# Two chained matrix products with a GELU between them: a first product opened by slices of the contraction, warm-up matmuls, and one load queue

## The chip, the cores and the metric

The kernel runs on one NeuronCore of a Trainium2 chip. The metric is the device time of one execution in microseconds. Three executions of the kernel before took 157.47, 232.58 and 156.98 us; their median is 157.47 us.

The engines by the names that the profile gives them: PE is TensorE (matmuls and transposes), with PEld for its loads of the stationary operand; DVE is VectorE, ACT is ScalarE, POOL is GpSimd, and SP issues DMAs (SPq is its queue). Matmuls write to PSUM, and DVE or ACT move their results from there to SBUF.

## The reference

```python
m, k, n, p = 1024, 1024, 2048, 1024     # a: m x k, b: k x n, c: n x p, all float32
h = np.matmul(a, b)
h = 0.5 * h * (1 + np.tanh(np.sqrt(2 / np.pi) * (h + 0.044715 * h ** 3)))
return np.matmul(h, c).astype(np.float32)
```

The inputs have 4.19 MB (a), 8.39 MB (b) and 8.39 MB (c); the output has 4.19 MB.

## The kernel before

All inputs come in as float32, are cast to bf16 on the core, and both products run in bf16 with sums in float32. One matmul multiplies a 128x128 stationary block by a 128x512 moving block. The first product has 16 column tiles of b (n), 8 slices of the contraction (k) and 1024 rows of a, so 16 x 8 x 2 = 256 matmuls; the second has 8 row tiles, 2 halves of the output's columns and 16 slices of its contraction, again 256.

The rows of a are worked in two chunks of 512 (the loop over mc). For each chunk `load_a_chunk` loads four row tiles of 128 x 1024 (tile sta, L51), casts them on ACT (a_bf, L53), and turns them by 64 transposes of 128x128 in the whole kernel (L60, by a matmul against an identity matrix) and as many DVE copies (L61) into aT, which has one 128x512 tile per slice of k. In the first chunk only, b is loaded in four slices of 512 columns, each as eight pieces of 128x512 (stb, L68) that ACT casts into b_sb (L69), and c comes in 16 row tiles (stc, L73, issued by POOL) that DVE casts (L74). For every column tile nt, eight matmuls (L90) sum one PSUM tile over k, and ACT applies the GELU and writes hT (L93). Then the second product runs over the chunk's four row tiles and two column halves: 16 matmuls (L100) sum one PSUM tile over all 16 tiles of hT, DVE copies it out (ot, L104) and SP stores it (L105). With that the chunk is done and the next one begins, with its own transposes.

The program is written in this order, but a scheduler places the instructions of each engine's queue: on PE it mixes transposes of one slice with matmuls of up to three open PSUM tiles. SP carries the loads of a and b and the stores; POOL carries those of c. Every load waits until its staging buffer (six each for sta and stb, three for stc) has been cast.

## Time and profile before

| what | value |
|---|---|
| three executions | 157.47, 232.58, 156.98 us (median 157.47) |
| span of the profiled execution | 157.0 us |
| mean granted TensorE clock | 0.946 |
| PE busy | 125.8 us (80%) |
| ACT busy | 47.6 us (30%) |
| DVE busy | 33.7 us (21%) |
| read from HBM, written | 20.97 MB, 4.19 MB |

The span runs from the first to the last instruction of one profiled execution on the one core. Nothing lies around it that the times show: it equals the lowest of the three times, 156.98 us, within its rounding. A row of a group of instructions gives the line, the engine, the operation, the tiles (out<-in), how often it ran, the busy time and the mean of one in ns, and then the idle time ahead of it with what ended it. A row of a stretch gives for each engine its busy microseconds and, in brackets, its instructions; then the granted clock as a share of full speed, the mean busy share of the 16 DMA engines and the GB/s that they moved. Matmuls overlap in their pipeline, so the mean duration of a matmul is longer than the time from one to the next.

### The profile page before, as it was taken

What the parts mean: (1) busy time and instruction counts of PE and PEld (TensorE: products, weight loads), DVE (VectorE), ACT (ScalarE), POOL (GpSimd) and SP (SyncE); (2) the same over time, 40 slices, a digit from 0 to 9 for tenths busy, and PEclk for the clock granted to TensorE, in tenths of its full rate; (3) what the DMA queues carried; (4) which work ended last, traced back from release to release, by engine and by line L of the source; (5) the groups of instructions that cost most, each with busy time, mean ns of one, the idle gap of its engine ahead of it and who ended that gap; (6) DMA issues with size and microseconds to landing.
All of it is one profiled execution on the core that took longest, in us unless ns stands there. A gap on an engine that the chain in (4) does not pass through costs nothing.

```text
span 157.0 us, 1522 instructions
## 1 busy us (share of the span) xinstructions
PE 125.8 (80%) x565; PEld 56.4 (36%) x576; DVE 33.7 (21%) x96; ACT 47.6 (30%) x74; POOL 9.3 (6%) x22
## 2 busy tenths in 40 slices
PE   0104952729994699999999979999999999999990
PEld 0001421213441244444444434444444444444440
DVE  0022664423113100011122146600000002111111
ACT  3534734497563995300000000053343310000000
POOL 6010121221210000000000000000000000000000
PEclk9999997555999789999999999999999999999999
DMA  5999999999999930011111120000000001122111
GB/s 177 406 381 316 362 338 413 397 399 401 395 399 398 410 155 2 0 67 71 67 67 69 69 103 30 0 4 0 0 0 0 0 4 67 67 84 112 72 67 67
DMA packets 10375, 25.26 MB, mean 161 GB/s; under 512 B 1152, under 2 KB 1152, under 8 KB 10368
## 3 DMA queue, kind: packets, MB, share of 16 engines
q1 hardware_dynamic: 8064, 16.78, 29.0%
q0 software_dynamic: 2304, 8.39, 13.6%
q8 instruction: 4, 0.07, 0.2%
q14 instruction: 3, 0.02, 0.1%
HBM read 20.97 MB, written 4.19 MB: 160 GB/s over the span
## 4 chain that ended last, share of the span: by engine, by line
PE 62%; DMA 26%; ACT 5%; DVE 2%; SPq 2%; issue 1%
PE ps L100 35%; DMA stb<-in_b_dram 26%; PE ps L90 24%; ACT b_sb L69 3%; PE pt L60 2%; ACT hT L93 2%; SPq L51 1%; DVE aT L61 1%; DVE ot L104 1%; ACT L93 1%; SPq L68 1%
## 5 line engine op out<-in xcount | busy, mean ns | idle before, releaser
L90 PE MATMUL ps<-aT,b_sb 128*128 128x512 bf16 x250 | 66.8, 410 | 8.9 <-ACT hT L93 7.1
L100 PE MATMUL ps<-c_sb,hT 128*128 128x512 bf16 x251 | 55.3, 379 | 0.3
L90 PEld LDWEIGHTS <-b_sb 128*128 128x128 bf16 x256 | 26.2, 103 | 48.7 <-issue 20.3
L100 PEld LDWEIGHTS <-hT 128*128 128x128 bf16 x256 | 25.0, 98 | 30.2
L93 ACT ACTIVATE hT<-ps 128x512 bf16<-128x512 f32 x32 | 18.6, 594 | 56.7 <-PE ps L90 55.6
L104 DVE COPY ot<-ps 128x512 f32<-128x512 f32 x16 | 11.1, 692 | 81.8 <-PE ps L100 81.8
L60 PE MATMUL pt<-ident,a_bf 128*128 128x128 bf16 x64 | 13.3, 240 | 18.4 <-ACT a_bf L53 11.7
L69 ACT ACTIVATE b_sb<-stb 128x512 bf16<-128x512 f32 x32 | 19.8, 629 | 15.1 <-DMA stb<-in_b_dram 14.8
L74 DVE CAST c_sb<-stc 128x1024 bf16<-128x1024 f32 x16 | 11.1, 692 | 27.2 <-DMA stc<-in_c_dram 27.1
L61 DVE COPY aT<-pt 128x128 bf16<-128x128 bf16 x64 | 12.5, 220 | 11.4 <-PE pt L60 10.8
L60 PEld LDWEIGHTS <-a_bf 128*128 128x128 bf16 x64 | 6.7, 107 | 17.7 <-ACT a_bf L53 12.3
L73 POOL DMA_DIRECT2D stc<-in_c_dram x16 | 8.6, 539 | 35.1 <-DVE aT L61 23.0
L53 ACT ACTIVATE a_bf<-sta 128x1024 bf16<-128x1024 f32 x8 | 8.4, 1054 | 6.3 <-DMA sta<-in_a_dram 6.3
L53 ACT ACT_TABLE_LOAD x1 | 1.3, 1283 | 0.7 <-PEq L120 0.7
L93 ACT ACT_TABLE_LOAD x1 | 1.3, 1283 | 0.0
masks.py:199 POOL TENSOR_SCALAR_AFFINE_SELECT ident<-ident 128x128 bf16<-128x128 bf16 x1 | 0.3, 306 | 0.1
masks.py:197 POOL MEMSET ident<- 128x128 bf16 x1 | 0.2, 205 | 0.3 <-POOLq L120 0.3
L120 POOL MEMSET const-float32-0.0<- 128x1 f32 x1 | 0.1, 99 | 0.2 <-issue 0.2
L120 POOL MEMSET const-bfloat16-1.0<- 128x1 bf16 x1 | 0.1, 102 | 0.0
L120 POOL MEMSET const-uint8-127<- 128x1 uint8 x1 | 0.1, 102 | 0.0
L120 POOL MEMSET const-float32-1.0<- 128x1 f32 x1 | 0.1, 99 | 0.0
## 6 DMA issues: line engine op xcount, KB each, us to landing
stc<-in_c_dram POOLq DMA_DIRECT2D x16, 512.0 KB, 6.8
stb<-in_b_dram SPq DMA_DIRECT2D x32, 256.0 KB, 7.5
sta<-in_a_dram SPq DMA_DIRECT2D x8, 512.0 KB, 7.9
out_dram<-ot SPq DMA_DIRECT2D x16, 256.0 KB, 2.0
```

The lines of the kernel that those rows point to most:

```text
L51: nc.sync.dma_start(out=st, in_=a[ds(mc * MC + mt * 128, 128), :])
L53: nc.scalar.activation(t, st, AF.Copy)
L60: nc.tensor.transpose(pt, a_bf[mt][:, ts(kt, 128)], ident)
L61: nc.vector.tensor_copy(at[:, ts(mt, 128)], pt)
L68: nc.sync.dma_start(out=st, in_=b[ts(kt, 128), ts(j, BS)])
L69: nc.scalar.activation(b_sb[kt][:, ts(j, BS)], st, AF.Copy)
L73: nc.gpsimd.dma_start(out=st, in_=c[ts(nt, 128), :])
L74: nc.vector.tensor_copy(c_sb[nt], st)
L90: nc.tensor.matmul(ps, b_sb[kt][:, ts(nt, 128)], aT[kt], start=(kt == 0), stop=(kt == KT - 1))
L93: nc.scalar.activation(h, ps, AF.Gelu_apprx_tanh)
L100: nc.tensor.matmul(ps, hT[nt][:, ts(mt, 128)], c_sb[nt][:, ts(pc, PC)], start=(nt == 0), stop=(nt == NT - 1))
L104: nc.vector.tensor_copy(ot, ps)
```

## The change

The kernel's body is rewritten, and the engines' queues now follow the written order (manual_schedule).

- The opening. a is loaded by slices of k: one DMA brings 128 columns of all 1024 rows (a_st, 512 KB, L64; the first slice in two halves, L60 and L62), followed by the same slice of the first 384 columns of b (b0_st, 192 KB, L65; the first of them on ACT's queue, L61). DVE casts the slice of a in two halves (L84, L85), ACT casts that of b (L86), PE makes eight transposes into two PSUM tiles of 128x512 (L90), and one wide copy each takes these to aT, on DVE for the first 512 rows (L92) and on ACT for the rest (L94). The function mm0 then adds this slice to six PSUM tiles at once (three column tiles by two halves of the rows, L79). All eight slices done, ACT applies the GELU to the six tiles (L120).
- The rest of the first product. mm1 works the column tiles 3 to 15, eight matmuls for each half of the rows (L126), with the GELU behind (L128). All of aT stays in SBUF, so both halves of the rows use a column tile of b when it is there. The second product starts when the first is done for all rows (L149); the last row tile's second half of columns is worked in two parts of 256.
- The loads. One queue, SP's, carries all loads but one in the order of use: the slices of the opening, b's column tiles 3, 4 and 5 singly (pieces of 128 columns), 6 and 7 together, 8 to 11, 12 to 15 (L107), then c by 1 MB (L113). DVE casts these (L108, L114), from four shared staging buffers of 1 MB.
- Ahead of it all DVE zeroes a tile (L45), PE makes seven matmuls of it that nothing reads (L73), and ACT runs one GELU on a column of it (L70).

How the queues change, at three places. The first is SP's queue from its start. A name such as a_st or sta is a staging tile, in_a_dram is the input a; the last numbers are the shape moved by one DMA. Before:

```order
L51 DMA sta<-in_a_dram 128x1024 x4
L68 DMA stb<-in_b_dram 128x512 x32
L51 DMA sta<-in_a_dram 128x1024 x4
L105 DMA out_dram<-ot 128x512 x16
```

Now, from the opening's second-last slice on:

```order
L64 DMA a_st<-in_a_dram 128x8x128
L65 DMA b_st<-in_b_dram 128x384
L64 DMA a_st<-in_a_dram 128x8x128
L65 DMA b_st<-in_b_dram 128x384
L107 DMA st<-in_b_dram 128x8x128 x3
L107 DMA st<-in_b_dram 128x8x256
L107 DMA st<-in_b_dram 128x4x512 x4
L113 DMA st<-in_c_dram 128x2x1024 x8
L142 DMA out_dram<-ot 128x512 x15
```

All of a now stands ahead of the wide loads of b, in pieces of 128 columns (512 bytes), and c's loads have moved from POOL's queue behind those of b.

The second place is PE's queue near the start; the weight load ahead of each matmul is left out. pt is a transposed block, ps a PSUM tile of the first product. Before, a block of four row tiles is turned and two or three sums are open:

```order
L60 MATMUL pt_156<-ident_58,a_bf_131 128x128
...
L90 MATMUL ps1_278<-aT_133,b_sb_93 128x512
...
L60 MATMUL pt_160<-ident_58,a_bf_119 128x128
...
L60 MATMUL pt_163<-ident_58,a_bf_123 128x128
...
L90 MATMUL ps1_264<-aT_146,b_sb_94 128x512
```

Now, behind the transposes of the second slice of k (aT0_1 is slice 0, second half of the rows; aT1_0 is slice 1, first half):

```order
L90 MATMUL pt_219<-ident_86,ab_209 128x128
...
L79 MATMUL ps_185<-aT0_1_92,b_sb_107 128x512
...
L79 MATMUL ps_187<-aT0_1_92,b_sb_107 128x512
...
L79 MATMUL ps_189<-aT0_1_92,b_sb_107 128x512
...
L79 MATMUL ps_184<-aT1_0_93,b_sb_107 128x512
...
L79 MATMUL ps_186<-aT1_0_93,b_sb_107 128x512
...
L79 MATMUL ps_188<-aT1_0_93,b_sb_107 128x512
```

Six sums are open, and each slice of a gives eight transposes and six matmuls; the three matmuls of the older slice stand between the transposes and the matmuls that need the newest copy.

The third place is DVE's queue, at the end of the opening. Before, the copies of single transposed blocks alternate with c's casts:

```order
L74 CAST c_sb<-stc 128x1024
L61 COPY aT<-pt 128x128 x4
L74 CAST c_sb<-stc 128x1024
L61 COPY aT<-pt 128x128
L74 CAST c_sb<-stc 128x1024 x9
```

Now the casts of a and one wide copy per slice, and behind them the casts of b and c:

```order
L84 CAST ab<-a_st 128x512
L85 CAST ab<-a_st 128x512
L92 COPY aT_0_105<-pt 128x512
L108 CAST b_sb<-st 128x8x128 x3
L108 CAST b_sb<-st 128x8x256
L108 CAST b_sb<-st 128x4x512 x4
L114 CAST c_sb<-st 128x2048 x8
```

No cast of c stands between the copies that PE waits for any more.

The added lines of the diff, cut to its core (the removed ones are the body printed above):

```diff
-    MC = 512
-    PC = 512
-    BS = 512
-    NSL = N // BS
+    MT = M // 128
+    H = 512
+    N0 = 3
+    W0 = N0 * 128
+    av = a.rearrange("(mt p) k -> p mt k", p=128)
+    bv = b.rearrange("(kt p) n -> p kt n", p=128)
+    cv = c.rearrange("(nt p) q -> p nt q", p=128)
+    ctx.enter_context(tc.manual_schedule())
     consts = ctx.enter_context(tc.tile_pool(name="consts", bufs=1))
-    ident = consts.tile([128, 128], BF16)
+    astage = ctx.enter_context(tc.tile_pool(name="astage", bufs=4))
+    abf = ctx.enter_context(tc.tile_pool(name="abf", bufs=3))
+    keep = ctx.enter_context(tc.tile_pool(name="keep", bufs=1))
+    b0stage = ctx.enter_context(tc.tile_pool(name="b0stage", bufs=4))
+    stage = ctx.enter_context(tc.tile_pool(name="stage", bufs=4))
+    opool = ctx.enter_context(tc.tile_pool(name="opool", bufs=4))
+    ppool = ctx.enter_context(tc.tile_pool(name="ppool", bufs=6, space=PSUM))
+    tpool = ctx.enter_context(tc.tile_pool(name="tpool", bufs=2, space=PSUM))
+    warm = consts.tile([128, H], BF16, name="warm")
+    nc.vector.memset(warm, 0.0)
+    ident = consts.tile([128, 128], BF16, name="ident")
     make_identity(nc, ident)
-    bpool = ctx.enter_context(tc.tile_pool(name="bpool", bufs=KT))
-    cpool = ctx.enter_context(tc.tile_pool(name="cpool", bufs=NT))
...
+    aT = [[keep.tile([128, H], BF16, name=f"aT{k}_{h}") for h in range(2)] for k in range(KT)]
+    b_sb = keep.tile([128, KT, N], BF16, name="b_sb")
+    c_sb = keep.tile([128, NT, P], BF16, name="c_sb")
+    hT = [[keep.tile([128, H], BF16, name=f"hT{t}_{h}") for h in range(2)] for t in range(NT)]
...
+    a_st, b_st = [], []
+    for k in range(KT):
+        st = astage.tile([128, MT, 128], F32, name="a_st")
+        bt = b0stage.tile([128, W0], F32, name="b0_st")
+        if k == 0:
+            nc.sync.dma_start(out=st[:, 0:4, :], in_=av[:, 0:4, ts(k, 128)])
+            nc.scalar.dma_start(out=bt, in_=bv[:, k, 0:W0])
+            nc.sync.dma_start(out=st[:, 4:8, :], in_=av[:, 4:8, ts(k, 128)])
+        else:
+            nc.sync.dma_start(out=st, in_=av[:, :, ts(k, 128)])
+            nc.sync.dma_start(out=bt, in_=bv[:, k, 0:W0])
+        a_st.append(st)
+        b_st.append(bt)
...
+    g = consts.tile([128, 1], F32, name="g")
+    nc.scalar.activation(g, warm[:, 0:1], AF.Gelu_apprx_tanh)
+    wps = tpool.tile([128, H], F32, name="pt")
+    for _ in range(7):
+        nc.tensor.matmul(wps, warm[:, 0:128], warm, start=True, stop=True)
...
+    ps = [[ppool.tile([128, H], F32, name="ps") for _ in range(2)] for _ in range(N0)]
...
+    def mm0(k, h):
+        for t in range(N0):
+            nc.tensor.matmul(ps[t][h], b_sb[:, k, ts(t, 128)], aT[k][h],
...
+    for k in range(KT):
+        ab = abf.tile([128, MT, 128], BF16, name="ab")
+        nc.vector.tensor_copy(ab[:, 0:4, :], a_st[k][:, 0:4, :])
+        nc.vector.tensor_copy(ab[:, 4:8, :], a_st[k][:, 4:8, :])
+        nc.scalar.activation(b_sb[:, k, 0:W0], b_st[k], AF.Copy)
+        for h in range(2):
+            pt = tpool.tile([128, H], BF16, name="pt")
+            for j in range(4):
+                nc.tensor.transpose(pt[:, ts(j, 128)], ab[:, 4 * h + j, :], ident)
+            if h == 0:
+                nc.vector.tensor_copy(aT[k][h], pt)
+            else:
+                nc.scalar.activation(aT[k][h], pt, AF.Copy)
+        if k > 0:
+            mm0(k - 1, 1)
+        mm0(k, 0)
+    mm0(KT - 1, 1)
...
+    def load_b(t0, nt):
+        w = nt * 128
+        kn = 2048 // max(w, 256)
+        for kh in range(0, KT, kn):
+            st = stage.tile([128, 2048], F32, name="st")
+            sv = st[:, 0:kn * w].rearrange("p (k n) -> p k n", k=kn)
+            nc.sync.dma_start(out=sv, in_=bv[:, kh:kh + kn, ds(t0 * 128, w)])
+            nc.vector.tensor_copy(b_sb[:, kh:kh + kn, ds(t0 * 128, w)], sv)
+    def load_c(t0):
+        st = stage.tile([128, 2048], F32, name="st")
+        sv = st.rearrange("p (t q) -> p t q", t=2)
+        nc.sync.dma_start(out=sv, in_=cv[:, t0:t0 + 2, :])
+        nc.vector.tensor_copy(c_sb[:, t0:t0 + 2, :], sv)
+    load_b(3, 1)
+    load_b(4, 1)
+    for h in range(2):
+        for t in range(N0):
+            nc.scalar.activation(hT[t][h], ps[t][h], AF.Gelu_apprx_tanh)
+    def mm1(t):
+        for h in range(2):
+            p = ppool.tile([128, H], F32, name="ps")
+            for k in range(KT):
+                nc.tensor.matmul(p, b_sb[:, k, ts(t, 128)], aT[k][h],
+                                 start=(k == 0), stop=(k == KT - 1))
+            nc.scalar.activation(hT[t][h], p, AF.Gelu_apprx_tanh)
+    load_b(5, 1)
+    load_b(6, 2)
+    load_b(8, 4)
+    load_b(12, 4)
+    for t in range(0, NT, 2):
+        load_c(t)
+    for t in range(N0, NT):
+        mm1(t)
...
+    def store(mt, q0, w, p):
+        ot = opool.tile([128, w], F32, name="ot", padded_shape=[128, H])
+        nc.vector.tensor_copy(ot, p)
+        nc.sync.dma_start(out=out[ts(mt, 128), ds(q0, w)], in_=ot)
+    for mt in range(MT):
+        h, j = divmod(mt, 4)
+        for q0, w in ((0, 512), (512, 512)) if mt < MT - 1 else ((0, 512), (512, 256), (768, 256)):
+            p = ppool.tile([128, w], F32, name="ps", padded_shape=[128, H])
+            for t in range(NT):
+                nc.tensor.matmul(p, hT[t][h][:, ts(j, 128)], c_sb[:, t, ds(q0, w)],
+                                 start=(t == 0), stop=(t == NT - 1))
+            store(mt, q0, w, p)
```

67 lines of the change are left out of this document (2 added, 65 removed).

## The prediction

> **What bounds the kernel now.** I read the page first, for where PE is not full, then the stretches between the breaks, then the chain of waits, for what holds each stretch.
>
> ```profile
> PE   0104952729994699999999979999999999999990
> DMA  5999999999999930011111120000000001122111
> PE 62%; DMA 26%; ACT 5%; DVE 2%; SPq 2%; issue 1%
> ```
>
> Each digit is a fortieth of the span, 3.9 us. PE is nearly full from the fourteenth slice on; before it, the DMA engines are full and PE is not.
>
> ```profile
> core 0: us, PE busy (x) PEld busy (x) DVE busy (x) ACT busy (x) POOL busy (x), PEclk, DMA share, GB/s
> 0.00:14.60 14.60, 1.53 (x6) 0.55 (x6) 1.76 (x7) 6.14 (x6) 2.92 (x10) 1.00 0.86 313
> 14.60:52.40 37.80, 25.37 (x104) 11.11 (x107) 14.65 (x41) 22.48 (x38) 6.35 (x12) 0.82 1.03 390
> 52.40:92.30 39.90, 39.74 (x175) 17.75 (x178) 4.87 (x8) 9.67 (x15) 0.00 (x0) 0.96 0.23 89
> 92.30:102.50 10.20, 8.80 (x54) 4.24 (x53) 6.92 (x33) 0.02 (x1) 0.00 (x0) 1.00 0.07 26
> ```
> ```profile
> 3.67 12.96 DMA stb<-in_b_dram
> ...
> 42.31 8.91 DMA stb<-in_b_dram
> ...
> 52.41 10.05 PE ps L90 x38
> ...
> 62.51 2.11 PE ps L90 x9
> 64.61 8.63 PE ps L100 x40
> ...
> 153.40 0.69 DVE ot L104
> ```
>
> The chain starts (3.67) on loads of b, stays on them with one interruption by a table load and GELUs, and turns to PE at 52.41. From there 47 matmuls of L90 are listed ahead of L100, 48 with one missing record. So of the first chunk's 128 matmuls only 80 were done in 52.4 us. The reason is what the load brings: with one half of a in place, each column tile of b (512 KB) gives PE just eight matmuls, and c fills half of the queue though nobody needs it yet. From 52.41 to 153.40 PE is almost gapless: 101.0 us for 48 + 128 + 256 = 432 matmuls and 32 transposes. The change must shorten the first 52 us; little is to be had behind.
>
> ```profile
> 149.95 0.69 DVE L104 COPY ot<-ps 128x512 f32<-128x512 f32 x1 [2.76 <-PE ps L100]
> 153.40 0.69 DVE L104 COPY ot<-ps 128x512 f32<-128x512 f32 x1 [2.76 <-PE ps L100]
> ```
>
> These give PE's price: 3.45 us from one copy to the next is 16 matmuls, 0.2156 us each.
>
> **The change part by part.** *The long stretch.* The opening does 3 x 2 x 8 = 48 matmuls; 208 + 256 = 464 remain, or 464 x 0.2156 = 100.0 us. That is 32 more than before's gapless stretch held (+6.9 us), but its 32 transposes, their waits (the stretch 92.3 to 102.5) and the half-clock start at 52.4 go (-7.9 us). The 256-wide matmuls of the last tile add nothing if they cost half.
>
> *The tail.* From 153.4 to 157.0 is 3.6 us: copy, store, end. The last copy and store are half as large. I take 0.35 us off the copy of 0.69 and 0.3 off the store: 3.0 us.
>
> *When the long stretch can start.* This is the open term. It is set by the bytes of the opening, 8 x (512 + 192) KB = 5.8 MB, and by what a 512-byte piece costs a DMA engine. No load of before has pieces that small; those of a had 4 KB, those of b 2 KB. Two stretches price them: the first has 4 KB alone, the second both.
>
> ```profile
> 51.50:55.50 4.00, 3.09 (x8) 1.09 (x8) 0.69 (x1) 4.00 (x8) 0.00 (x0) 0.64 1.03 409
> 30.00:50.00 20.00, 15.51 (x57) 6.17 (x57) 5.32 (x8) 13.79 (x23) 3.19 (x7) 0.78 1.04 399
> q1 hardware_dynamic: 464, 1.63, 103.0%
> q0 software_dynamic: 1129, 4.15, 52.8%
> q1 hardware_dynamic: 2093, 3.81, 50.9%
> ```
>
> First: 1.63 MB is 398 pieces, and 16 engines x 4.0 us / 398 = 161 ns each. Second: 4.15 MB is 1013 pieces of 4 KB, 163 us of the 320 engine-us; the other 157 us went to 3.81 MB, 1860 pieces of 2 KB, 84.5 ns each. A straight line through 161 and 84.5 has a fixed part of 8 ns and 38 ns per KB: 27 ns for 512 bytes. Lower bound: bytes alone, 161/8 = 20 ns. Upper bound: a small piece costs what a 2 KB one costs, 84.5 ns. I take 28 ns, by the line and just above it, since it is read outside its ends. An engine has 64 pieces of a slice of a, 1.79 us, and 8 rows of 1.5 KB of b, 8 x 66 ns = 0.53 us: 2.3 us a slice, 18.6 us for eight.
>
> ```profile
> 0.00:2.00 2.00, 0.00 (x0) 0.00 (x0) 0.00 (x0) 1.26 (x1) 1.07 (x6) 1.00 0.23 27
> 2.00:4.00 2.00, 0.00 (x0) 0.00 (x0) 0.00 (x0) 0.02 (x1) 1.32 (x3) 1.00 0.86 336
> out_dram<-ot SPq DMA_DIRECT2D x16, 256.0 KB, 2.0
> L68 SPq DMA_DIRECT2D stb<-in_b_dram x32: 327/328/530, 2.6 to 46.8; - x32
> ```
>
> By 4.0 us 0.73 MB had moved, 1.8 us at 409 GB/s: the loads run as if from 2.2 us. A store lands 2.0 us after its issue, 0.64 of them for its bytes; of the rest I give 0.3 to the end. So the opening's loads land by 2.2 + 18.6 + 0.3 = 21.1 us. SP's issues, 16 x 0.33 to 0.53 us, hide behind them if an issue's price doesn't grow with its pieces. A slice's next load waits for the cast of the slice four before; with three slices (6.9 us) in flight that wait is hidden.
>
> *The engines beside it.*
>
> ```profile
> L69 ACT ACTIVATE b_sb<-stb 128x512 bf16<-128x512 f32 x32 | 19.8, 629 | 15.1 <-DMA stb<-in_b_dram 14.8
> L93 ACT ACTIVATE hT<-ps 128x512 bf16<-128x512 f32 x32 | 18.6, 594 | 56.7 <-PE ps L90 55.6
> L104 DVE COPY ot<-ps 128x512 f32<-128x512 f32 x16 | 11.1, 692 | 81.8 <-PE ps L100 81.8
> L74 DVE CAST c_sb<-stc 128x1024 bf16<-128x1024 f32 x16 | 11.1, 692 | 27.2 <-DMA stc<-in_c_dram 27.1
> 94.21 0.22 PE L60 MATMUL pt<-ident,a_bf 128*128 128x128 bf16 x1
> 94.27 0.38 PE L90 MATMUL ps<-aT,b_sb 128*128 128x512 bf16 x1
> ```
>
> DVE has two casts of 512 (half of 692, 0.35 each) and one copy of 512 from PSUM (at most 0.69): 1.4 us a slice. ACT has a cast of 384 (under 0.63) and a copy (0.6): 1.2 us. PE: a transpose holds it 0.06 us (94.21 to 94.27), 0.22 if nothing overlaps; four in a row I put at 0.1: 8 x 0.1 + 6 x 0.2156 = 2.1 us a slice (bounds 1.8 and 3.1). All are below 2.3, so the loads pace the opening, by little. Behind the last loads: a's slice lands 0.5 us before b's, at 20.6; two casts (0.7), four transposes behind the second of them (0.4) and the nine matmuls still open (1.9) put PE's end at 23.6. Column tile 3 lands 1.8 us after 21.1, its cast (1024 wide) takes 0.7: 23.6 again. The first GELU has freed its PSUM tile by about 23.2. **Start of the long stretch: 23.6 us.** Tiles 4 and 5 come 1.8 us apart, while a tile keeps PE busy 3.45: no gap. The rest (5.2 MB of b, 8.4 of c, at 399 GB/s 34 us) is in by 62 us with its cast; c is needed at 23.6 + 13 x 3.45 = 68.5. That cover of 6 us is gone if the loads run below some 335 GB/s, and each us then costs one.
>
> *Sum:* 23.6 + 100.0 + 3.0 = 126.6 us, against 52.4 + 101.0 + 3.6 = 157.0 of the profiled execution, which is 0.3% under the median of 157.47. I forecast **126.6 us**.
>
> The warm-up matmuls end before the first slice is there and cost nothing unless they are late: seven at half clock (0.43 each) are 3.0 us, from about 1.0 to 4.0.
>
> The Trainium skill, "DMA: Bandwidth & Descriptors", "Why small descriptors are slow (HBM only)", speaks against the 512-byte pieces: each packet pays some 3 cycles beside its 32-byte beats. By that, as an estimate, 512 bytes cost 161 x 19/131 = 23 ns against 20 for bytes alone, a slice 2.0 us, and the sum would be 124, the first rival's. No run so far shows pieces this small.
>
> **The rivals.** *1. PE paces the opening.* For it: the lower bound of 20 ns makes 1.8 us a slice, and up to 24 ns it stays under PE's 2.1. The first slice is there at about 4.2, eight slices take 16.8, the start is at 21: 124.0 us. Against it: the 27 ns of the line.
>
> *2. Small pieces are half as fast as by the line, or the issue is paid by pieces.* At 42 ns a slice takes 2.7 + 0.5 us, eight 25.7, and tile 3 comes 2.7 + 0.7 later: start 31.6, 134.6 us. SP paying 0.33 us per 128 pieces gives nearly the same, 8 x 0.33 + 0.33 = 3.0 us a slice. The trace has no row against it.
>
> *3. The clock drops in the opening.*
>
> ```profile
> 14.60:18.50 3.90, 3.85 (x16) 1.90 (x17) 1.90 (x9) 2.42 (x4) 0.53 (x1) 1.00 1.05 407
> 18.50:22.00 3.50, 2.49 (x19) 1.41 (x18) 2.83 (x12) 2.14 (x5) 1.06 (x2) 1.00 0.98 287
> 24.00:27.40 3.40, 0.97 (x7) 0.49 (x7) 1.34 (x6) 1.61 (x3) 0.53 (x1) 0.70 1.03 410
> 27.40:30.80 3.40, 2.97 (x8) 1.14 (x9) 1.36 (x5) 1.26 (x2) 1.05 (x2) 0.50 1.04 396
> ```
>
> After 0.97 us of work in 3.4 PE was at 0.50, at 71% busy (2.49 of 3.5) it stayed at full clock. The opening has PE at 90%, and a gap only before the first slice. If it starts cold, PE needs 6 x 0.43 + 8 x 0.13 = 3.6 us a slice for the 4 to 5 us until the clock returns, falls some 2 us behind and gets most of it back slowly: 128.5 us. The Trainium skill, "TensorE: Matmul & The Clock Gate", "Part 1: The HAM clock gate", says that about 3.4 us of activity open the gate, in a window that runs freely; seven matmuls of 3.0 us would then not always do. The trace agrees as far as it goes: in the two rows from 14.6 us on, PE took 3.85 us for 16 instructions and then 2.49 for 19, so it grew faster after some 3.9 us of work, though the clock column reads 1.00 in both.
>
> *4. Slower than before: a piece costs as much as a 2 KB one.* Place: the DMA queue, where a, tiles 3 to 5 and 6-7 have 64 small pieces per engine and 512 KB (for 6-7, 1 MB). At 84.5 ns a slice takes 5.9 us, the opening 47.5 (landed at 50.0), tile 6 lands 21.6 later and is cast 1.4 later, at 73; from there 10 x 3.45 + 256 x 0.2156 + 3.0 = 92.7: 165.7 us. It decides from about 73 ns (157 us). For it speaks only that nothing smaller was measured; against it that 2 KB pieces cost half of 4 KB ones.
>
> **How the numbers follow.** Forecast 0.44 (126.6, own range 125 to 129), rival 1 0.2, rival 2 0.24, rival 3 0.07, rival 4 0.03, and 0.02 for no change, by a gap that I overlooked in the long stretch. The range is 122.5 to 136. Below it there is little room: 512 matmuls are 110.4 us, 64 transposes at 0.06 are 3.8, the first slice comes at about 4, the tail is 3, together 121.2. Above it lie rival 2 beyond 45 ns a piece, and rival 4. About 2% either way can be told from no change here. Faster 0.95, the same 0.02, slower 0.03.
>
> **What would show it.** Right: loads of a_st landing 2.3 us apart, the first L126 matmul near 23.6, the second product (L149) near 68.5 with no wait for c, PE gapless to the last copy. Wrong in its size: slices 3 us or more apart (rival 2), or PE never waiting for a cast in the opening (rival 1), or a granted clock of 0.5 behind 5 us (rival 3). Wrong as a whole: the first L126 later than 52 us, or breaks between 24 and 124.

## The result, and the profile after

The changed kernel takes 132.14 us (median of 4 executions, 132.01 to 132.35) against 157.77 us before (median of 4, with the one of 232.58 us): a ratio of 0.8385 with a 95% interval of 0.8335 to 0.8436. The forecast was 126.6 us, so 5.75 us are missing against the profiled execution of 132.35 us. Its span is 130.6 us, its mean clock 0.987. Disturbed executions are left out of the ratios: one of the four before (232.58 us) and, of the runs below, two of four with 1 KB pieces (187.08 and 446.43 us, the profiled one among them), two of four with the queue's order alone (156.29 and 156.82 us) and the profiled one of the second repair (136.18 us).

First the page: a slice is now 3.3 us, and the third line is the share of the chain of waits that ended last.

```profile
PE   6479998879999999999999999999999999999990
DMA  2999999999999999999000022221111222222231
PE 77%; DMA 16%; DVE 2%; SPq 1%; ACT 0%; issue 0%; DVEq 0%
```

PE is at 70% or more from the fourth slice on, where before it was nearly full from the fourteenth on. The loads still fill the first half of the span, but from the fourth slice on PE works beside them. The chain of waits (start, duration, what) shows where what is left of the start goes, and then nothing but PE:

```profile
9.12 6.23 DMA a_st<-in_a_dram
...
18.33 7.76 DMA st<-in_b_dram
26.09 0.02 issue
26.11 0.70 DVE b_sb L108
26.81 0.05 issue
26.86 45.07 PE ps L126 x208
71.93 55.31 PE ps L149 x272
```

Read it from the end. The two products are one gapless stretch, 45.07 + 55.31 = 100.38 us. It starts at 26.86, not at 23.6 as forecast, and what released it is the load of column tile 3. The loads ahead of it are a's. What the opening looked like is in the stretches (us, then PE, PEld, DVE, ACT and POOL busy with their counts, the granted clock, the DMA share, GB/s):

```profile
2.00:4.00 2.00, 2.00 (x6) 0.60 (x4) 0.00 (x0) 0.67 (x2) 0.00 (x0) 1.00 0.71 115
...
8.00:10.00 2.00, 1.56 (x11) 0.98 (x10) 1.19 (x3) 0.70 (x3) 0.00 (x0) 0.50 1.16 306
10.00:12.00 2.00, 2.00 (x9) 0.80 (x8) 0.76 (x2) 1.10 (x2) 0.00 (x0) 0.66 1.14 302
...
18.00:20.00 2.00, 1.74 (x14) 0.96 (x14) 0.96 (x3) 1.12 (x2) 0.00 (x0) 1.00 1.16 309
```

In these rows the loads move 302 to 309 GB/s once they run, but only 115 from 2 to 4 us. PE is at 0.50 from 8 us on, in spite of the seven warm-up matmuls, and recovers. The last two slices and the first two column tiles on DVE (one row is one instruction; the bracket is the idle time ahead of it and what ended it), and the last cast of b's slices on ACT:

```profile
20.10 0.43 DVE L84 CAST ab<-a_st 128x512 bf16<-128x512 f32 x1 [0.98 <-DMA a_st<-in_a_dram]
...
22.43 0.43 DVE L84 CAST ab<-a_st 128x512 bf16<-128x512 f32 x1 [0.99 <-DMA a_st<-in_a_dram]
...
26.11 0.69 DVE L108 CAST b_sb<-st 128x1024 bf16<-128x1024 f32 x1 [2.33 <-DMA st<-in_b_dram]
27.74 0.69 DVE L108 CAST b_sb<-st 128x1024 bf16<-128x1024 f32 x1 [0.94 <-DMA st<-in_b_dram]
```
```profile
22.92 0.52 ACT L86 ACTIVATE b_sb<-b_st 128x384 bf16<-128x384 f32 x1 [0.97 <-DMA b_st<-in_b_dram]
```

Slices are 22.43 - 20.10 = 2.33 us apart, each waited for by DVE: the loads pace the opening. Tile 3 lands 26.09 - 22.90 = 3.2 us behind the last slice of b, tile 4 only 1.6 us behind tile 3. PE's own account of that is the idle time in its group of the column tiles:

```profile
L126 PE MATMUL ps<-aT,b_sb 128*128 128x512 bf16 x208 | 45.1, 379 | 1.3 <-DVE b_sb L108 1.3
L149 PE MATMUL ps<-c_sb,hT 128*128 128x512 bf16 (+1 forms) x272 | 55.5, 366 | 0.0
```

1.3 us of idle, all of it for tile 3's cast; the second product waits for nothing. So the opening's matmuls ended at about 25.6, and tile 3 kept PE for 1.3 us more.

### The profile page after: what moved, and what is told of

Same layout as the page of the kernel before. It is cut to its first block, busy times and chain, and to the rows that moved or that the text cites. A ratio compares the mean times of both kernels' runs of the same rounds, so it can differ in the third digit from the quotient of the medians.

```text
span 130.6 us, 1457 instructions
## 1 busy us (share of the span) xinstructions
PE 120.7 (92%) x599; PEld 56.1 (43%) x599; DVE 39.0 (30%) x58; ACT 29.0 (22%) x50; POOL 0.7 (1%) x6
## 4 chain that ended last, share of the span: by engine, by line
PE 77%; DMA 16%; DVE 2%; SPq 1%; ACT 0%; issue 0%; DVEq 0%
PE ps L149 42%; PE ps L126 35%; DMA a_st<-in_a_dram 10%; DMA st<-in_b_dram 6%; SPq L65 1%; DVE ab L84 1%; PE pt L90 1%; DVE b_sb L108 1%; ACT aT L94 0%; SPq L62 0%; SPq L60 0%; DVE ot L141 0%; DVE ab L85 0%; DVEq L84 0%
## 5 line engine op out<-in xcount | busy, mean ns | idle before, releaser
L149 PE MATMUL ps<-c_sb,hT 128*128 128x512 bf16 (+1 forms) x272 | 55.5, 366 | 0.0
L126 PE MATMUL ps<-aT,b_sb 128*128 128x512 bf16 x208 | 45.1, 379 | 1.3 <-DVE b_sb L108 1.3
L149 PEld LDWEIGHTS <-hT 128*128 128x128 bf16 x272 | 26.6, 98 | 28.9
L126 PEld LDWEIGHTS <-b_sb 128*128 128x128 bf16 x208 | 20.3, 98 | 26.1 <-DVE b_sb L108 1.8
L141 DVE COPY ot<-ps 128x512 f32<-128x512 f32 (+1 forms) x17 | 11.2, 660 | 51.5 <-PE ps L149 51.5
L128 ACT ACTIVATE hT<-ps 128x512 bf16<-128x512 f32 x26 | 15.5, 597 | 29.4 <-PE ps L126 29.4
L114 DVE CAST c_sb<-st 128x2048 bf16<-128x2048 f32 x8 | 9.8, 1227 | 10.7 <-DMA st<-in_c_dram 10.7
L79 PE MATMUL ps<-aT,b_sb 128*128 128x512 bf16 x48 | 12.7, 402 | 0.0
L108 DVE CAST b_sb<-st 128x2048 bf16<-128x2048 f32 (+1 forms) x8 | 8.2, 1027 | 12.4 <-DMA st<-in_b_dram 12.4
L90 PE MATMUL pt<-ident,ab 128*128 128x128 bf16 x64 | 6.1, 232 | 4.0 <-DVE ab L84 3.5
L90 PEld LDWEIGHTS <-ab 128*128 128x128 bf16 x64 | 4.0, 102 | 8.9 <-DVE ab L84 7.4
L84 DVE CAST ab<-a_st 128x512 bf16<-128x512 f32 x8 | 3.4, 427 | 10.8 <-DMA a_st<-in_a_dram 10.8
L79 PEld LDWEIGHTS <-b_sb 128*128 128x128 bf16 x48 | 4.6, 103 | 4.4 <-issue 0.8
L86 ACT ACTIVATE b_sb<-b_st 128x384 bf16<-128x384 f32 x8 | 4.2, 523 | 8.2 <-DMA b_st<-in_b_dram 8.2
L94 ACT ACTIVATE aT<-pt 128x512 bf16<-128x512 bf16 x8 | 4.8, 597 | 4.5 <-PE pt L90 4.5
L73 PE MATMUL pt<-warm 128*128 128x512 bf16 x7 | 3.2, 630 | 1.2 <-DVE warm L45 1.2
L92 DVE COPY aT<-pt 128x512 bf16<-128x512 bf16 x8 | 3.4, 423 | 1.9 <-PE pt L90 1.9
L85 DVE CAST ab<-a_st 128x512 bf16<-128x512 f32 x8 | 3.4, 420 | 0.5 <-DMA a_st<-in_a_dram 0.5
L120 ACT ACTIVATE hT<-ps 128x512 bf16<-128x512 f32 x6 | 3.0, 615 | 0.3 <-PE ps L79 0.3
L73 PEld LDWEIGHTS <-warm 128*128 128x128 bf16 x7 | 0.9, 140 | 2.6 <-issue 1.4
L45 DVE MEMSET warm<- 128x256 uint32 x1 | 0.3, 272 | 0.9 <-PEq L166 0.9
```

What stands on the lines that cost most here:

```text
L73: nc.tensor.matmul(wps, warm[:, 0:128], warm, start=True, stop=True)
L79: nc.tensor.matmul(ps[t][h], b_sb[:, k, ts(t, 128)], aT[k][h], start=(k == 0), stop=(k == KT - 1))
L84: nc.vector.tensor_copy(ab[:, 0:4, :], a_st[k][:, 0:4, :])
L86: nc.scalar.activation(b_sb[:, k, 0:W0], b_st[k], AF.Copy)
L90: nc.tensor.transpose(pt[:, ts(j, 128)], ab[:, 4 * h + j, :], ident)
L94: nc.scalar.activation(aT[k][h], pt, AF.Copy)
```

## The experiments

Two theories of the opening stood at first. P: the loads pace it, at 28 ns for a piece of 512 bytes, and the rest of the miss is sizes. I: SP's issues pace it (an issue of b's slice takes SP 1.34 to 2.53 us in the changed kernel, in the median 1.71, against 0.33 to 0.53 for b's loads before). What PE waits for at 25.6 us, tile 3's late landing, has theories of its own, with other letters, in the expectations. The ratios are all to the kernel before, run on the same chip.

### Who issues b's slices

```diff
-            nc.sync.dma_start(out=bt, in_=bv[:, k, 0:W0])
+            nc.gpsimd.dma_start(out=bt, in_=bv[:, k, 0:W0])
```

> The opening's slices of b, seven of eight, are issued by POOL instead of SP; the bytes and the pieces are the same. In the profile of the change each of these issues held SP for 1.3 to 2.5 us behind a load of a with 1024 pieces, and an issue of a plus one of b add up to the 2.3 us between slices. Theory P: the DMA engines were the limit and SP was only held back by them; the slices stay 2.3 us apart and the time 132.1 within 0.7. Theory I: SP was the limit; without b's issues the slices come 2.0 us apart or less and the time falls by 2 us or more, to 130 or below.

Measured: 131.99 us (131.81 to 132.06), ratio 0.8352. DVE's rows of the last two slices in this run:

```profile
20.46 0.43 DVE L84 CAST ab<-a_st 128x512 bf16<-128x512 f32 x1 [0.65 <-DMA a_st<-in_a_dram]
...
22.80 0.43 DVE L84 CAST ab<-a_st 128x512 bf16<-128x512 f32 x1 [0.99 <-DMA a_st<-in_a_dram]
```

Still 2.34 us apart with seven issues taken off SP. I falls: SP's long issues do not set the pace. That the time is the change's as well is partly chance. Tile 3 is there at 24.5 us in this run (the table further down shows why), and the long stretch starts 0.9 us earlier:

```profile
25.96 8.85 PE ps L126 x41
```

But its span ends 4.0 us behind the start of the last copy (126.18 to 130.2), against 3.3 in the change (127.26 to 130.6). Why its end takes longer is open.

### Wider pieces

a is loaded in pairs of slices, 1 KB a piece, each pair in two halves:

```diff
-        st = astage.tile([128, MT, 128], F32, name="a_st")
...
-            nc.sync.dma_start(out=st, in_=av[:, :, ts(k, 128)])
+        if k % 2 == 0:
+            st2 = astage.tile([128, MT, 256], F32, name="a_st")
+            nc.sync.dma_start(out=st2[:, 0:4, :], in_=av[:, 0:4, ts(k // 2, 256)])
...
+            nc.sync.dma_start(out=st2[:, 4:8, :], in_=av[:, 4:8, ts(k // 2, 256)])
```

> a is loaded by 256 columns in pieces of 1 KB, two slices of k per pair of loads; b's slices, the order on PE and all else stay. Theory P prices a piece of 1 KB by the line of the prediction at 46 ns against 2 x 28: a pair of slices takes 64 x 46 + 16 x 66 = 4.0 us instead of 4.7, the eight 16.0 instead of 18.6, the last landing comes 2 to 3 us earlier, and the time falls to about 130. Theory I (SP's issuing paces the opening: 0.4 us for a load of a and 1.7 us for the load of b behind it) expects hardly less, since SP now issues as many loads or more: 131.5 to 133. A theory that PE's own chain paces it expects 132 as well.

Measured: 129.81 and 130.02 us, ratio 0.8223 (0.8159 to 0.8286); there is no trace of either. As P expected, the same bytes of a in half as many pieces take less time, 2.2 us less than the change.

### No warm-up matmuls

```diff
-    wps = tpool.tile([128, H], F32, name="pt")
-    for _ in range(7):
-        nc.tensor.matmul(wps, warm[:, 0:128], warm, start=True, stop=True)
```

> The changed kernel without its seven warm-up matmuls. In the profile of the change the granted clock read 0.50 from 8 to 10 us and 0.66 from 10 to 12 us although the warm-ups ran, and the slices still came 2.33 us apart from the third on. Theory P (the loads pace the opening, by what their 512-byte pieces cost) expects no difference: 132.1 us within 0.5, with PE at half clock until some 12 to 13 us as before, and the first matmul of column tile 3 within 0.3 us of 26.9. A theory that the warm-ups carry the clock (rival 3 of the prediction) expects about 2 us more, 134, with the half clock lasting to 15 us or later.

Measured: 130.79 us (130.69 to 130.88), ratio 0.8276 (0.8227 to 0.8325). That is 1.35 us faster than the changed kernel (whose interval begins at 0.8335), and P's expectation missed it. So did the theory that the warm-ups carry the clock, which expected 134. DVE's queue shows where:

```profile
22.35 0.43 DVE L81 CAST ab<-a_st 128x512 bf16<-128x512 f32 x1 [0.98 <-DMA a_st<-in_a_dram]
...
24.64 0.69 DVE L105 CAST b_sb<-st 128x1024 bf16<-128x1024 f32 x1 [0.95 <-DMA st<-in_b_dram]
27.81 0.69 DVE L105 CAST b_sb<-st 128x1024 bf16<-128x1024 f32 x1 [2.47 <-DMA st<-in_b_dram]
```

The slices are where they were (22.35 against 22.43). But tile 3 is there at 24.6, and now tile 4 is the late one, 3.2 us behind it. The long stretch starts at 25.51; tile 3 is 3.45 us of work for PE, past the end of tile 4's cast at 28.50, so PE waits for nothing. So taking seven matmuls out of PE's queue moved a delay of some 1.4 us from one load to the next, although the loads and their order are the same.

### Tile 3 alone in its staging buffer

```diff
+    tstage = ctx.enter_context(tc.tile_pool(name="tstage", bufs=1))
...
-            st = stage.tile([128, 2048], F32, name="st")
+            st = (tstage if nt == 1 else stage).tile([128, 1024 if nt == 1 else 2048], F32, name="st1" if nt == 1 else "st")
```

Tiles 3, 4 and 5 share one buffer, so nothing is in the queue behind tile 3 until it has been cast.

> Column tiles 3, 4 and 5 of b share one staging buffer, so that the load of tile 4 and all behind it on SP wait until tile 3 is cast. In the change tile 3 landed 3.2 us after the opening's last slice, where its bytes at the opening's rate take 1.7. Theory R (the engines run ahead: without a wait behind it the loads of tiles 4 to 7 are worked by some engines while others still owe tile 3): tile 3 lands about 1.8 us after the last slice, its first matmul comes 1.0 to 1.4 us earlier, near 25.6, limited by the end of the opening on PE; tile 4 then comes late, so the time stays within 132 to 134. Theory S (pieces of b, 8 KB apart, are slower than those of a): tile 3 lands 3 us after the last slice as before and tile 4 another 4 to 5 us later, and the time rises by 1 to 3 us.

Measured: 135.34 us (134.93 to 135.53), ratio 0.8562, slower since tiles 4 and 5 now come late themselves. What it was made for is the stretch from 22 to 27 us, in 40 parts of 0.125 us (first the DMA engines' mean busy share in tenths, then GB/s):

```profile
DMA  9999999998759200000000001000000000000000
GB/s 303 311 332 299 303 283 295 287 242 213 168 139 242 66 4 0 0 0 0 0 0 8 8 8 12 0 0 0 0 0 0 0 0 0 0 0 0 0 0 0
```

The flow of tile 3 ends at 23.8, and then, alone, a last trickle of 8 to 12 GB/s comes at 24.6 to 25.1; the cast starts at 25.79. R is refuted, since tile 3 is late with nothing behind it in the queue. S's times nearly came out (tile 4 is cast 4.8 us after tile 3, the kernel is 3.2 us slower), but not its reason: the flow runs near 300 GB/s and stops. A load is spread over 16 DMA engines, and one of them delivers its part late.

That one part can be seen. The trace notes for every load 16 landings, one for each engine. Worked out from these, with the start and duration of a fetch of instructions (16 KB, a queue of its own, q8) that the next section puts down to PE:

```
kernel                     fetch         load     first  fifteenth  sixteenth landing (us)
the change                 23.80, 1.21   b, k=7   21.69   22.77     22.90
                                         tile 3   23.51   24.68     26.09
                                         tile 4   25.25   26.42     27.72
without warm-ups           25.40, 1.22   tile 3   23.64   24.60     24.62
                                         tile 4   25.45   26.40     27.78
tile 3 alone               23.52, 1.17   tile 3   23.64   24.29     25.77
b's slices issued by POOL  23.65, 1.21   tile 3   23.69   24.34     24.50
                                         tile 4   25.40   26.23     27.59
```

In each of them all parts but one of a load land within 1.2 us, and from the first or second tile after the start of the fetch on, the sixteenth comes 1.3 to 1.5 us behind the fifteenth. In the loads that land ahead of the fetch it never does: there the sixteenth is at most 0.12 us behind in the change, 0.09 without warm-ups, 0.21 where POOL issues. It stays behind while the queue is full: without warm-ups by 1.46 to 1.47 us in every load from 29.6 us to the next fetch, at 47.66. With tile 3 alone, where the queue runs empty, the load of tile 4 has no such part any more (0.05 us). A tile whose part on that engine is in by then is spared, as tile 3 is where POOL issues. The lag is least plain in the kernel of pairs without warm-ups (below): its sixteenth part is 0.5 to 0.6 us behind from the start on, the fetch comes at 23.74, and the late load is tile 5, 27.56 against 26.60, two loads on. The profile has the fetch in its list of queues; for the change, from 23.5 to 24.5 us, and for the kernel without warm-ups, from 25.2 to 26 us (packets, MB, share of 16 engines):

```profile
q8 instruction: 1, 0.02, 7.6%
```
```profile
q8 instruction: 1, 0.02, 9.5%
```

7.6% of 16 engine-us is 1.2 us: one engine for 1.2 us, the size of the lag.

### Warm-up matmuls of eight columns

Theory F: a fetch of PE's instructions takes one DMA engine, and the count of instructions ahead decides when. Theory W: the warm-ups' work on PE decides. Seven matmuls remain, but of eight columns instead of 512:

```diff
-        nc.tensor.matmul(wps, warm[:, 0:128], warm, start=True, stop=True)
+        nc.tensor.matmul(wps[:, 0:8], warm[:, 0:128], warm[:, 0:8], start=True, stop=True)
```

> The changed kernel with its seven warm-up matmuls cut to 8 columns each: PE runs the same number of instructions, but the warm-up work is gone. Without the warm-ups the time was 130.8, and tile 3 landed at 24.6 instead of 26.1. Theory F (one DMA engine is held for 1.2 us by a fetch of 16 KB of PE's instructions, which comes when PE has worked off a fixed number of them; with the warm-ups it comes at 23.8 us, while tile 3 is being loaded, without them at 25.4, when tile 4 is, which has slack): the count is the same, so tile 3 is late again: 132.1 within 0.4. Theory W (the work of the warm-ups itself costs): 130.8 within 0.4.

Measured: 132.18 us (132.13 to 132.32), ratio 0.8351: no difference to the change. Tile 3's cast and the long stretch:

```profile
25.91 0.69 DVE L108 CAST b_sb<-st 128x1024 bf16<-128x1024 f32 x1 [2.46 <-DMA st<-in_b_dram]
```
```profile
26.66 45.07 PE ps L126 x208
```

With hardly any warm-up work but all of its instructions, the fetch starts at 23.21 us and tile 3 is late again (sixteenth part at 25.89, fifteenth at 24.34). W falls, F holds. How far PE's queue was when the fetch began can be read from the stretch up to it, in the change, without warm-ups and with the eight columns (the second count is PEld's, one weight load for each matmul or transpose):

```profile
0.00:23.80 23.80, 18.58 (x112) 8.62 (x113) 9.76 (x25) 9.96 (x18) 0.70 (x6) 0.93 1.03 269
```
```profile
0.00:25.40 25.40, 17.63 (x111) 8.66 (x113) 10.47 (x26) 11.37 (x20) 0.70 (x6) 1.00 1.05 269
```
```profile
0.00:23.21 23.21, 16.27 (x111) 8.37 (x112) 9.52 (x25) 9.85 (x17) 0.70 (x6) 1.00 1.04 270
```

112 or 113 weight loads each time, at 23.21 to 25.40 us: that speaks for a count of PE's instructions, not for a time. In versions with another order on PE the count is between 80 and 116. No run is without the fetch; the evidence is this count, and that the late load follows the fetch from kernel to kernel.

### The queue's order alone, in the kernel before

```diff
-        nc.gpsimd.dma_start(out=st, in_=c[ts(nt, 128), :])
+        nc.sync.dma_start(out=st, in_=c[ts(nt, 128), :])
...
-                if mc == 0:
-                    load_c(nt)
...
+        if mc == 0:
+            for nt in range(NT):
+                load_c(nt)
```

> The kernel before with one part of the change alone: c is loaded on SP's queue behind all of b, instead of by POOL beside it; chunks of 512 rows, transposes, casts and the opening stay as they were. Theory O (the order of the loads is most of the gain): b is in by 2.2 us + 10.5 MB at 400 GB/s = 28.4 us, the first product of the first chunk ends near 40, c is in by 49.5, the first chunk's second product ends near 74.5 instead of 92.3, and the rest takes 64.8 us as before: a span of 139, a time of about 141. Theory H (the gain comes from both halves of the rows being ready for each tile of b): with c out of the way the first chunk only waits for c instead of b, and the time stays above 152.

Measured: 153.92 us in the profiled execution (span 152.1), 153.62 to 156.82 in all four, ratio 0.9714 (0.9635 to 0.9792). Theory O, that the order alone brings most of the gain, is refuted by 13 us. The stretch in which b should have come, and then the chain of waits:

```profile
22.00:24.00 2.00, 1.88 (x9) 0.87 (x9) 0.00 (x0) 2.00 (x6) 0.00 (x0) 1.00 0.76 218
24.00:26.00 2.00, 2.00 (x11) 0.80 (x9) 0.00 (x0) 2.00 (x5) 0.00 (x0) 1.00 0.56 153
```
```profile
50.81 4.74 DMA stc<-in_c_dram
...
56.30 4.40 DMA stc<-in_c_dram
...
61.45 4.76 DMA stc<-in_c_dram
66.23 0.70 DVE c_sb L74
66.97 20.46 PE ps L101 x86
```

PE is busier early, as wanted. But ACT, full with GELUs and with b's casts in one queue (2.00 of 2 us), now frees b's buffers late, and the loads fall to 153 GB/s. Then c comes through three buffers: three tiles of 0.52 MB in 4.7 + 0.7 us, 290 GB/s, so it is in at 66 us, and PE waits. The order alone is worth 3%, 4.5 us: the wait went from b to c.

### c beside the opening, in the changed kernel

```diff
+    def load_c(t):
+        st = cstage.tile([128, P], F32, name="stc")
+        nc.gpsimd.dma_start(out=st, in_=c[ts(t, 128), :])
+        nc.vector.tensor_copy(c_sb[:, t, :], st)
...
+        load_c(k)
```

The first eight row tiles of c come on POOL's queue, one for each slice of the opening, through three buffers.

> The changed kernel with the one queue undone: c is loaded by POOL in 16 row tiles of 512 KB beside the opening and b, with three staging buffers as in the kernel before, one cast per slice of the opening on DVE, the rest behind b's. Theory Q (the order of use is worth what c's bytes take in the opening): 8 to 11 of c's row tiles, 4 to 5.8 MB, come in beside the opening's 5.8 MB, which then takes 10 to 14 us longer at 310 to 400 GB/s: the first matmul of tile 3 near 38, a time of 142 to 147. A theory that the order of the loads hardly matters once both halves of the rows are at work expects under 135.

Measured: 147.21 us (145.56 to 147.26), ratio 0.9318 (0.926 to 0.9375). Two slices late in the opening, and the long stretch:

```profile
21.94 0.43 DVE L90 CAST ab<-a_st 128x512 bf16<-128x512 f32 x1 [1.70 <-DMA a_st<-in_a_dram]
...
25.50 0.43 DVE L90 CAST ab<-a_st 128x512 bf16<-128x512 f32 x1 [1.62 <-DMA a_st<-in_a_dram]
```
```profile
39.54 46.75 PE ps L127 x208
```

Slices are 3.56 us apart instead of 2.33, and the long stretch starts 12.7 us later. Theory Q, that c's bytes take their share of the engines, gave 142 to 147 us; the time is at its upper end. DVE's casts of c stand between the slices, but they do not hold it up: from 21.9 us on each slice's cast still waits 1.6 to 1.7 us for its own load. So the order of the loads is worth some 15 us here and 4.5 in the old structure. I read the difference so: here each byte of the opening gives PE work at once, there PE ran into ACT's queue and c's three buffers.

### a by whole rows

4 KB pieces instead of 512 bytes: the eight row tiles of a first, then b's eight slices; DVE casts and copies a row tile at a time.

```diff
+    for mt in range(MT):
+        st = astage.tile([128, K], F32, name="a_st")
+        nc.sync.dma_start(out=st, in_=a[ts(mt, 128), :])
+        a_st.append(st)
...
+    for mt in range(MT):
+        turn(mt)
```

> The changed kernel with a loaded by whole rows (pieces of 4 KB, all eight row tiles first), then b's eight slices of 384 columns; the accumulation over k in six PSUM tiles, the rest and the warm-ups stay. Theory P: a takes 8 x 8 x 161 ns = 10.3 us instead of 14.5, the loads start as if from 2.2 us instead of 3.2, so the first slice of b is cast at 13.9 and from there PE has work without a wait: 48 matmuls end at 24.3 against 25.6 and no gap for tile 3 follows, 129.5 us; 131.5 if PE's clock is still half at 13.9. A theory that overlapping the opening's loads with matmuls is what the slices gain expects the loss of that overlap to weigh more: 133 or above.

Measured: 137.44 us (137.26 to 137.54), ratio 0.8684, 8 us above what P expected. Its DVE queue, and two stretches of its windows:

```profile
9.55 0.68 DVE L77 CAST ab<-a_st 128x1024 bf16<-128x1024 f32 x1
10.94 0.42 DVE L85 COPY aT<-pt 128x512 bf16<-128x512 bf16 x1 [0.70 <-PE pt L81]
11.28 0.68 DVE L77 CAST ab<-a_st 128x1024 bf16<-128x1024 f32 x1
```
```profile
18.00:20.00 2.00, 0.90 (x5) 0.28 (x3) 0.27 (x1) 1.73 (x5) 0.00 (x0) 1.00 0.00 0
20.00:22.00 2.00, 2.00 (x6) 0.74 (x5) 0.00 (x0) 0.51 (x2) 0.00 (x0) 1.00 0.74 211
...
24.00:26.00 2.00, 2.00 (x11) 0.91 (x10) 0.00 (x0) 1.05 (x2) 0.00 (x0) 1.00 0.95 270
```

The loads are fast, but two things that the slices hide come out. DVE's queue is in order: cast, wait 0.70 for PE's transposes, copy, next cast, 1.73 us a row tile where the load needs 1.3 (8 x 161 ns). ACT's casts of b stand behind its copies of aT until 18.8, so b's four buffers come free late, and from 18 to 20 us nothing moves at all. And all 48 matmuls come after the last transpose: they start at 19.3 with a slow PE, 6 in 2 us against 11 later.

### Two repairs of it: six column tiles, one half of the rows at a time

```diff
-    N0 = 3
+    N0 = 6
...
+    for mt in range(4):
+        load_a(mt)
...
+        nc.sync.dma_start(out=bt, in_=bv[:, k, 0:W0])
+    for mt in range(4, MT):
+        load_a(mt)
```

The upper four row tiles, then b's slices 768 wide (3 KB pieces), then the lower four.

> A version built on theory P: first the upper 512 rows of a by whole rows, then b's slices 768 columns wide (pieces of 3 KB), into six PSUM tiles of the upper rows, then the lower 512 rows of a, whose transposes stand between; then the six tiles of the lower rows, and all the rest as in the change. Matmuls can start at 9.2 us, the lower rows are ready near 22, and from there PE is gapless: a span of 125.6, a time of about 127.4. If the matmuls start at half clock, or the lower rows land late, 128 to 130. Without the gain from larger pieces it would be no better than 132.

Measured: 135.25 us (134.43 to 136.2), ratio 0.8546, 8 us above what P expected. Its first matmuls of the product run at half clock, and the clock drops a second time, after the lower rows were turned with PE 0.92 of 2 us busy (26 to 28 us):

```profile
12.00:14.00 2.00, 1.98 (x5) 0.73 (x6) 1.20 (x3) 0.09 (x1) 0.00 (x0) 0.50 0.72 246
...
30.00:32.00 2.00, 2.00 (x7) 0.63 (x5) 0.29 (x2) 0.00 (x0) 0.00 (x0) 0.52 1.04 385
```

The second repair puts each cast ahead of the copy on DVE, gives half of b's casts to ACT, six buffers to b's slices, and extra matmuls to keep PE's clock up:

```diff
+        if nxt is not None:
+            cast(nxt)
...
+    def fill(n):
+        w = tpool.tile([128, H], F32, name="pt")
+        for _ in range(n):
+            nc.tensor.matmul(w, warm[:, 0:128], warm, start=True, stop=True)
```

> The version with whole rows and six column tiles again, with what held it back removed: the cast of a row tile now stands ahead of the copies of the one before on DVE's queue (they took turns before, 1.73 us a tile, where the load takes 1.3), half of b's casts go to ACT, six staging buffers instead of four for b's slices, and eight added matmuls that nothing reads stand among the transposes so that PE's clock stays up. Theory P: with the loads as the pace again, matmuls start near 10 and the lower rows are ready near 22 us; a span of 126, a time of about 128. If DVE or the clock still pace it, 130 to 134.

Measured: 135.47 us (133.99 to 136.18), ratio 0.8567. It changed nothing. In the profiled execution PE was at 0.50 from 10 to 18 us all the same, and the long stretch began at 30.4; but that execution is the slowest of the four, with a mean clock of 0.962, and two others took 135.45 and 135.49 us at 0.998 and 0.999. Slow starts of PE and late buffers are what the traces of the rows show; which of the two weighs more these runs don't tell.

### Wider pieces without warm-ups, and a mixed version

The pairs of slices, with no warm-up matmuls (both diffs above together):

> The two edits that helped, together: a by 256 columns in pieces of 1 KB, and no warm-up matmuls. Theory P (the loads pace the opening): a pair of slices takes 4.0 us instead of 4.7, the opening's loads end 2 to 3 us earlier than in the change; with pieces of 1 KB alone the undisturbed runs took 129.8 and 130.0. Theory F (PE's instruction fetch hits the load that is in flight): the fetch comes some 1.5 us later than with the warm-ups, so the gap ahead of tile 3, if there is one, may go or come: between 128.5 and 130.0. If the warm-ups matter for the clock once the loads are faster: 130.5 or above.

Measured: 130.23 us (130.22 to 130.54), ratio 0.827, just above what was expected. A window in the middle of the opening and the chain:

```profile
14.00:16.00 2.00, 2.00 (x18) 1.18 (x16) 1.35 (x4) 1.12 (x3) 0.00 (x0) 1.00 1.09 359
```
```profile
24.97 44.89 PE ps L123 x208
```

The loads now run at 349 to 360 GB/s from 8 to 20 us and PE is full: the first rival of the prediction, PE pacing the opening, at 1.74 us a slice from 13.5 us on. But PE starts late, on its first pair at 7.72 us against 6.22 in the change, and slowly: eight transposes take 1.06 us at first and 0.61 from 13.5 us on.

That led to the last kernel: the first and the last slice alone (short wait at the start, short rest at the end), six in pairs between, and eleven warm-up matmuls so that PE's idle time ahead of the first slice is short.

```diff
+    for k0, w in ((0, 1), (1, 2), (3, 2), (5, 2), (7, 1)):
+        st = astage.tile([128, MT, w * 128], F32, name="a_st", padded_shape=[128, MT, 256])
+        nc.sync.dma_start(out=st[:, 0:4, :], in_=av[:, 0:4, ds(k0 * 128, w * 128)])
...
-    for _ in range(7):
+    for _ in range(11):
```

> With pieces of 1 KB and no warm-ups PE waited for the first pair of slices until 7.7 us and then paced the opening itself, at half clock until near 14. Here the first and the last slice of a come alone in pieces of 512 bytes, the six between in pairs with pieces of 1 KB, and eleven warm-up matmuls instead of none reach to about 6 us, where the first slice is cast. If the first slice's landing and PE's clock were what bound that version, PE's opening ends about 1 us earlier than its 24.97 and the time is 128.5 to 129.5. If PE's work at full clock with its waits binds (1.74 us a slice was measured), eight slices from 6.2 end at 21 and the loads bind again: last landing near 21.8, end of the opening near 24, the same 129. If PE's instruction fetch, earlier by some 2 us now, holds one of the last slices: 130 to 130.5.

Measured: 129.50 us (six executions, 129.03 to 130.42), ratio 0.8269 (0.8232 to 0.8306). The long stretch:

```profile
23.97 44.89 PE ps L127 x208
```

It is 17% under the kernel before, and 2% under the change by the medians (129.50 against 132.14; 1.4% by the ratios, whose intervals don't overlap). That it is the best version is not shown: its median is the lowest, but the ratio of the kernel with 1 KB pieces is lower (0.8223), and its own interval overlaps those of the kernels with 1 KB pieces, without warm-ups, and with both. The clock stays at 1.00 from 4 to 22 us, and the fetch comes at 22.0 us, which makes tile 4 late instead of tile 3 (sixteenth part at 25.91, fifteenth at 24.58). What of the 2.6 us is the pieces', the clock's and the fetch's part was not separated.

## Why the prediction was right or wrong

- **What bounded the kernel before, and what the change does to it: right.** The first 52 us were the place; the long stretch begins at 26.86 now, and no break follows.
- **The price of a 512-byte piece, 28 ns: right.** In the row of 18 to 20 us the loads run at 309 GB/s, so a slice of 0.72 MB takes 2.33 us (2.3 forecast). 16 engines by 2.33 are 37.3 engine-us; less 128 rows of b at 66 ns, 28.9 for 1024 pieces, 28.2 ns. With 1 KB pieces, at 355 GB/s by the windows of the run without warm-ups (349 to 360), the same working gives 4.06 us a pair, 65 - 17 = 48 engine-us for 1024 pieces, 47 ns; the line has 46. The Trainium skill, "DMA: Bandwidth & Descriptors", "Why small descriptors are slow (HBM only)", gives by its 3 cycles a packet the 23 ns estimated in the prediction; the measurement decides against it, 28.2 ns, and with it against the first rival.
- **When the loads begin: wrong by 1.0 us.** "The loads run as if from 2.2 us" was read from 4 KB pieces (336 GB/s from 2 to 4 us). The change has 115 GB/s in that row: 0.26 MB by 4.0 us, 0.8 us' worth at 309, so as if from 3.2. The run with whole rows had 381 GB/s there, the others with small pieces 94 (1 KB) to 144 (eight-column warm-ups). These differ from the rows in one thing more: b's first slice is loaded on ACT's queue at the same time, and of the 0.23 MB that the change moves from 2 to 4 us 0.15 are b's. So the slow start is shown, but not whether the small pieces or the second queue make it.
- **The last landing: wrong by 0.8 us.** I gave 0.3 us behind the bytes. The 16 parts of the last slice land from 21.69 to 22.90, spread over 1.2 us, and a cast needs them all. Together with the start, the last slice is in at 22.90 instead of 21.1.
- **PE behind the last slice: right.** 2.5 us forecast (21.1 to 23.6), some 2.7 measured (22.90 to about 25.6).
- **Tile 3 hidden: wrong by 1.3 us, and the one step whose mechanism was missing.** Fifteen parts land at 24.68, 1.8 us behind the slice, just as forecast. The sixteenth is held by the instruction fetch until 26.09. The prediction had no term for it. The page of the kernel before lists the fetches (q8, 4 packets, 0.07 MB), but nothing on it tells what they cost.
- **The long stretch, 100.0 us: right** (100.38), and c's cover too: the last cast of c starts at 63.71 us, and the second product begins at 71.93.

```profile
63.71 1.23 DVE L114 CAST c_sb<-st 128x2048 bf16<-128x2048 f32 x1 [1.26 <-DMA st<-in_c_dram]
```

- **The tail, 3.0 us: 0.3 short** (127.24 to 130.56).
- **The time around the span: forgotten, 1.75 us.** I took the span of the kernel before, 157.0, for its time, because it met the lowest of the times shown. It must have been another execution's: in every run that has both, the time is 1.7 to 2.4 us above the span (132.35 and 130.6; before, 156.67 and 154.9). So 126.6 was a forecast of a span.

The sum of it: 1.0 + 0.8 + 0.2 + 1.3 = 3.3 for the start, 0.4 for the stretch, 0.3 for the tail and 1.75 around the span are the 5.75 us between 126.6 and 132.35. The time lies inside the range of 122.5 to 136, but outside the forecast's own 125 to 129. None of the rivals came about: PE waited for the slices (against 1), the price of a piece was the line's (against 2 and 4). The clock did drop to 0.50 from 8 us on, as rival 3 says, but with the loads pacing the opening PE had the time to spare: DVE still waited 0.98 and 0.99 us for the last two slices. The Trainium skill, "TensorE: Matmul & The Clock Gate", "Part 1: The HAM clock gate", has the clock judged in windows of about 3.4 us: the trace agrees, the half clock lasts from 8.0 to 11.4 us (a mean of 0.66 from 10 to 12 us is 1.4 us at half), 3.4 us, behind the window with the 1.86 us of idle time after the warm-up matmuls:

```profile
6.22 0.40 PE L90 MATMUL pt<-ident,ab 128*128 128x128 bf16 x4 [1.86 <-DVE ab L84]
```

## What to carry to other kernels

Price an opening that the loads pace by pieces, not bytes (here 28 ns for 512 bytes and 47 for 1 KB on one DMA engine), and try wider pieces: the three versions with pieces of 1 KB took 129.5 to 130.2 us against 132.1. That narrow first and last slices help beside them was not shown. What moving loads into the order of use brings depends on what waits next: 15 us in this structure, 4.5 in the old one, where the wait went on to the next buffer. Where one load in a row is late by an odd microsecond, look whether one of its sixteen parts is, and what else that DMA engine did; and compare the time with the span before a sum is made.

## What the runs showed of the hardware that was not expected

- A fetch of 16 KB, which comes with the count of PE's instructions, holds one of the 16 DMA engines for 1.2 us and lets the load in flight land 1.3 to 1.5 us late, and the loads behind it too while the queue is full. Removing seven matmuls moved it past tile 3, and the kernel was 1.35 us faster; shrinking them to eight columns was worth nothing.
- On one engine a piece costs 28 ns at 512 bytes, 47 at 1 KB, 84.5 at 2 KB and 161 at 4 KB: close to 8 ns and 38 ns per KB (the first two are worked out with b's rows beside them at the prediction's 66 ns).
- Between 2 and 4 us the loads move 94 to 144 GB/s where the first pieces of a have 512 bytes or 1 KB and b's first slice comes on a second queue, and 336 to 381 where they have 4 KB.
- A copy of 128x512 bf16 from PSUM by DVE takes 0.42 us, less than the 0.69 that I allowed from a copy of float32.
- The clock column can read 1.00 where the spacing shows a slow PE: 6 matmuls in 2 us (20 to 22 us, a by whole rows) against 11 from 24 us on. The first clock that the trace of that run notes is at 23.4 us, 1.00.
- In the profiled executions, seven warm-up matmuls and then 1.86 us of idle time left PE at half clock from 8.0 to 11.4 us; eleven, with 0.84 us of idle time behind them, left it at 1.00.
